# A hybrid decoder step on one core: the rotation in pieces of 256 columns, and the border to the feed-forward part regrouped

## The chip, the core and the metric

The kernel runs on one core of one Trainium2 chip. The metric is the device time of one execution in microseconds. Before the change it is 2496.76 us, the median of three runs (2495.86 to 2498.49). One further execution was taken with the hardware profiler; all rows below come from it.

## The reference

One layer of an autoregressive decoder, for a prompt of 1024 tokens and eight single-token samples with the same weights. Columns are tokens here: 1032 of them, cut into two halves of 516 where the halves matter. What bears on the change:

```
proj = rmsnorm(x, g_mix) @ w_in
rq, rk = rotary(rq, pos), rotary(rk, pos) * RET_DK ** -0.5     # 4 heads of 128
o_r, s_ret = retention_chunked(rq, rk, rv, s_ret)
...
x = x + merged @ w_out
x = x + cross_attn(rmsnorm(x, g_x), mk, mv, w_xq, w_xo)
h = rmsnorm(x, g_ffn)
x = x + (silu(h @ w_gate) * (h @ w_up)) @ w_down
```

`rotary` takes the two halves x1, x2 of a head's 128 channels to x1 cos - x2 sin and x1 sin + x2 cos. `rmsnorm` scales each token by 1 / sqrt(mean of squares + eps), which the kernel computes as exp(-0.5 ln(...)).

## The kernel before, in words

Every large product is made of three TensorE products: each float32 operand is split into a high part (ScalarE copies it to a shorter format, `L235`, `L253`) and a low part (the remainder, formed by VectorE or GpSimd, `L236`, `L254`). `dense` (`L252` to `L254` in `wsplit`) loads 512 KB of weights through SP's queue into a staging tile, splits it, and multiplies block by block; a function called `evac` brings each block out of PSUM.

The stages follow each other: the input projections with the gated-delta branch, then the retention branch together with projections and the memory keys and values, then `w_out` with the residual, cross attention, `w_xo` with the second residual, the feed-forward part, and the final norm. TensorE's order in the first stages is written out by hand: dense products call `tick()`, which lets threads of the other branches put in their products when a simulated clock says so. On the other engines a planner orders the instructions by a simulated timeline; every engine then works its queue in order. `tc.issue_after(ins)` ties what a block issues on the engine of `ins` behind `ins`, and nothing else.

**The rotation.** `ret_qk(h, u)` loads queries and keys of one head and one half of 512 tokens into `qk` ([128, 2, 512], `rqk` in the rows). `swapped` (`L887`) multiplies each half of the partitions by the sine rows into the other half of `w` (`rsw`), two instructions of 64 partitions; `L904` multiplies `qk` by the cosines and `L905` adds `w`. All four run on GpSimd, for 2 x 512 columns at a time, for each of eight units. Low halves of the rotated queries (`L928`) and of the scores (`L936`) are formed on GpSimd as well. Beside that VectorE carries the samples' retention and gated-delta states (`svn`, `L1151` to `L1161`), the retention state's low halves (`rS`), evacuations (`ev`, `kv`) and weight remainders.

**The tables of ScalarE.** A norm is `rsnorm`: a product with ones on TensorE (`pn`), Ln (`L315`) and Exp (`L317`) on ScalarE, block by block. ScalarE needs the table of a function loaded; `preload_act_table_set("natural_log_exp_and_others")` asks for the set that has both, once at the start (`L211`) and once ahead of `residual(w_out)` (`L1402`). The latter has no operands, so nothing ties its place in ScalarE's order.

**The border to the feed-forward part.** `residual_half(c, ms)` (`L1545` on) multiplies by `w_xo`, tile by tile of 128 rows, for half c of the tokens. Its evacuation adds the old x (`L1558`), stores the sum, squares it (`L1561`), adds the squares up on GpSimd (`L1563`) and multiplies x by the gain in place (`L1564`), which waits for the store. The feed-forward products use a seven-product scheme on quarters: `xr[r][c]` is rows half r, token half c, as two tiles each. `scale(r, c)` (`L1571`) multiplies a quarter by the norm `rsB`, two instructions of 128x1032. `operands(p, ...)` splits the sums or differences that product p needs.

```
        residual_half(0, range(KT))
        rsnorm(rsB, sqx, D, halves_of(0))
        residual_half(1, range(2))
        with tc.issue_after(taken[0].ins):      # the last evacuation traced
            scale(0, 0)
        operands(1, r2tile, quarters(0, 0))
        scale(1, 0)
        operands(2, r2tile, quarters(1, 0))
        residual_half(1, range(2, KT))
```

`Pair(ft)` is one tile of 128 hidden rows: it loads gate and up weights (`wg`, `wu`; `wraw` takes the staging tile from the rotating list `stage`), forms sums of their quarters on GpSimd (`L1687`, numbers 5, 6, 7 and, last, 3, which overwrites the sum of number 6), and `product(p)` splits the weights and issues 24 TensorE products and their evacuations (`L1717` to `L1736`). Tiles 0 and 1 run their products in the order 1, 2 (tile 0), 1, 2 (tile 1), 7, 7, 5, 6, 6, 4, 4, 3, 5, 3. Behind the first of these the second half's norm is issued; then the quarters of half 1 are scaled (`L1773`), their difference `xt3` for product 7 is formed (`L1774`), and the further differences (`L1779`) and operands follow, all ahead of product 7 in the program. Tiles 2 to 21 follow with all seven products each.

Of the kernel before, what the change touches and what calls it, by code (L numbers as in the profile page):

```python
# [9 lines left out]
F32 = mybir.dt.float32  # L10
F32R = mybir.dt.float32r
AF = mybir.ActivationFunctionType
ALU = mybir.AluOpType
# [4 lines left out]
P = 128  # L18
# [4 lines left out]
KT = D // P  # L23
# [3 lines left out]
H = NT // 2  # L27
# [116 lines left out]
def build(tc, io):  # L144
    nc = tc.nc
    ve, se, ge = nc.vector, nc.scalar, nc.gpsimd
# [19 lines left out]
    with ExitStack() as es:  # L166
# [11 lines left out]
        wp = pool("wp", 2)  # L178
# [49 lines left out]
        def r1tile(name, dt=F32R):  # L228
            return r1p.tile([P, NT], dt, name=name, tag="r1")
# [13 lines left out]
        stage = [wp]  # L243
# [640 lines left out]
        def swapped(w, t, r):  # L884

            for o, i in ((slice(0, 64), slice(64, P)), (slice(64, P), slice(0, 64))):
                ge.tensor_tensor(w[o], t[i], r[i], op=ALU.mult)  # L887
# [8 lines left out]
        def ret_qk(h, u):  # L896
            n = f"{h}_{u}"
            cs = slice(u * 512, u * 512 + 512)
            qk = rp.tile([P, 2, 512], F32, name=f"rqk{n}", tag="rqk", bufs=2)
            w = rp.tile([P, 2, 512], F32, name=f"rsw{n}", tag="rsw")  # L900
            load(qk, rqkd[:, h:h + 5:4, cs], h + u == 1)
            rots = [rot[:, j, cs].unsqueeze(1).to_broadcast([P, 2, 512]) for j in range(2)]
            swapped(w, qk, rots[1])
            ge.tensor_tensor(qk, qk, rots[0], op=ALU.mult)  # L904
            ge.tensor_tensor(qk, qk, w, op=ALU.add)  # L905
            return qk

        def ret_v(h, u):
# [490 lines left out]
                one(m)  # L1399
            return oh, ol  # L1400

        se.preload_act_table_set("natural_log_exp_and_others")  # L1402
        sqx = e2.tile([P, NT], F32, name="sqx", tag="sqx", bufs=1)
        xh, xl = residual(io["w_out"], gh, gl_, lambda m: io["xT"][:, m], x1d, G_X, lambda m: r2tile, sqx, "x1")
        rsB = cp.tile([P, NT], F32, name="rsB1", tag="rsB")
# [133 lines left out]
        def pair(new, name, dt=F32R):  # L1539
            return new(name, dt).rearrange("p (i t) -> p i t", i=2)  # L1540
# [39 lines left out]
        def operands(p, new, srcs):  # L1580
            xo[p] = []
            for j, s in enumerate(srcs):
                t = pair(new, f"xo{p}_{j}")
                split(t[:, 0], t[:, 1], s)
                xo[p].append(t)
# [1 line left out]
        quarters = lambda r, c: [quarter(r, c, j) for j in range(4)]  # L1587
        residual_half(0, range(KT))
        rsnorm(rsB, sqx, D, halves_of(0))
        residual_half(1, range(2))  # L1590

        with tc.issue_after(taken[0].ins):
            scale(0, 0)
        operands(1, r2tile, quarters(0, 0))
        scale(1, 0)
        operands(2, r2tile, quarters(1, 0))
        residual_half(1, range(2, KT))
        ast.close()

        pss.close()  # L1600
# [8 lines left out]
        def ftile(tag, name, shape, bufs=1, dt=F32):  # L1609
            return fp.tile(shape, dt, name=name, tag=tag, bufs=bufs)  # L1610

        stage[:] = [wp, fp, fp, fp]
        nop = [0]

        def wop(name):
# [49 lines left out]
        class Pair:  # L1665


            def __init__(self, ft):
                self.ft = ft
                wg, wu = wraw(f"wg{ft}"), wraw(f"wu{ft}")  # L1670
                dma(out=wg, in_=io["w_gate"][ft])
                flush(dma(out=wu, in_=io["w_up"][ft]))
                a11, a12, a21, a22 = wg[:, :4], wg[:, 4:], wu[:, :4], wu[:, 4:]
                s1, s2 = (ftile(f"S{i}", f"S{i}_{ft}", [P, 4, P], 2) for i in (1, 2))
                self.srcs = {1: a11, 2: a12, 3: s2, 4: a22, 5: s1, 6: s2, 7: a21}
                self.sums = {5: (s1, a21, a22, ALU.add), 6: (s2, s1, a11, ALU.subtract), 7: (a21, a11, a21, ALU.subtract),
                             3: (s2, a12, s2, ALU.subtract)}
                self.at, self.seen = {}, []
                self.t = r1tile(f"hid{ft}", F32)
                up = ev if ft % 2 else e1  # L1680
                self.U = [up.tile([P, BLK], F32, name=f"U{ft}_{i}", tag="ev" if ft % 2 else "gt")[:, :H // 2] for i in range(2)]

            def weights(self, p):
                for q in {6: (5, 6), 7: (5, 7), 5: (5,), 3: (5, 6, 3)}.get(p, ()):
                    if q in self.sums:
                        o, x, y, op = self.sums.pop(q)
                        ge.tensor_tensor(o, x, y, op=op)  # L1687
                w = wop(f"w{p}_{self.ft}")
                split(*w, self.srcs[p])
                return w  # L1690
# [75 lines left out]
        f1 = Pair(1)  # L1766
        for p in (1, 2):
            f1.product(p)
        xt3 = [pair(r1tile, f"xt3{i}", F32) for i in range(2)]
        for i in range(2):  # L1770
            for r in (1, 0):
                e = xr[r][1][i]
                ve.tensor_tensor(e, e, rsB[:, half(1)].unsqueeze(1).to_broadcast([P, 2, H]), op=ALU.mult)  # L1773
            ve.tensor_tensor(xt3[i], xr[1][1][i], xr[0][1][i], op=ALU.subtract)  # L1774
        operands(7, r2tile, [xt3[j // 2][:, j % 2] for j in range(4)])
        for p, new, (r, c) in ((5, r2tile, (0, 1)), (6, r1tile, (0, 1)), (4, r1tile, (1, 0))):
            for i in range(2):
                x, y = (xr[r][c][i], xr[0][0][i]) if p == 5 else (xr[1][1][i], xr[0][1][i]) if p == 6 else (xr[1][0][i], xr[0][1][i])
                ve.tensor_tensor(xr[r][c][i], x, y, op=ALU.subtract)  # L1779
            operands(p, new, quarters(r, c))  # L1780
        operands(3, r1tile, quarters(1, 1))
        for f, p in ((f0, 7), (f1, 7), (f0, 5), (f0, 6), (f1, 6), (f0, 4), (f1, 4), (f0, 3), (f1, 5), (f1, 3)):
            f.product(p)
        f0.done()
        f1.done()
# [143 lines left out]
```

## Time and profile before, and how to read it

| | |
|---|---|
| median of three runs | 2496.76 us |
| the profiled execution | 2501.62 us |
| its span, first to last instruction | 2499.8 us |
| mean granted TensorE clock | 0.986 |
| instructions | 44199 |
| busy: TensorE / VectorE / ScalarE / GpSimd | 2401.3 / 1518.8 / 978.2 / 897.6 us |
| read from HBM, written | 243.91 MB, 97.78 MB |

PE is TensorE, DVE VectorE, ACT ScalarE, POOL GpSimd, SPq the queue of loads and stores. Products are pipelined, so TensorE's busy time counts overlaps, and a busy TensorE is not one at its peak; the granted clock (PEclk, 1.00 is 2.4 GHz, 0.50 is 1.2 GHz) says how fast it could run. `L157` is the line of every TensorE product, so products are told apart by their tiles: `pd` is a dense product, `P` one of the feed-forward scheme, `pks`, `pro`, `prs` are of the retention stage, `pn` is a norm. A wait is given as idle time of the engine and what released it.

### The profile page before, as it was taken

How to read it: one execution, taken by the hardware profiler on the slowest of the kernel's cores; microseconds unless marked ns; L12 is line 12 of the kernel's file. 1: busy time of each engine (PE TensorE's matmuls, PEld its weight loads, DVE VectorE, ACT ScalarE, POOL GpSimd, SP SyncE). 2: the span in 40 equal slices, each digit the busy share in tenths (PEclk: the TensorE clock that was granted, in tenths of full speed). 3: DMA queues.
4: the chain of work that ended last, by engine and by line, in shares of the span. 5: the costliest groups of instructions: out<-in, count | busy, mean ns of one | idle time of the engine just before them, and what ended most of it. 6: DMA issues, size and time to landing. Idle time of an engine off the chain costs nothing. (4 is left out here: it accounts for less than half of the span.)

```text
span 2499.8 us, 44199 instructions
## 1 busy us (share of the span) xinstructions
PE 2401.3 (96%) x17290; PEld 2314.2 (93%) x17290; DVE 1518.8 (61%) x2957; ACT 978.2 (39%) x1757; POOL 897.6 (36%) x846
## 2 busy tenths in 40 slices
PE   8999999999999999898999999998889999999998
PEld 6999999999999998788999999878889999999998
DVE  5866857668576536787544445342496656656665
ACT  4333243433424333564422343234543333335453
POOL 4344243343434327442001120003388655620233
PEclk9999999999999999999999999999989999999999
DMA  4222222222222236577666543335345445438654
GB/s 145 87 68 72 89 89 85 72 74 86 82 84 76 83 112 197 194 227 233 212 184 177 157 135 102 124 126 177 107 136 189 162 131 170 140 126 286 211 157 150
DMA packets 201090, 344.60 MB, mean 138 GB/s; under 512 B 39984, under 2 KB 125488, under 8 KB 200752
## 3 DMA queue, kind: packets, MB, share of 16 engines
q1 hardware_dynamic: 200880, 341.76, 43.5%
q8 instruction: 136, 2.23, 0.4%
q14 instruction: 74, 0.61, 0.1%
HBM read 243.91 MB, written 97.78 MB: 137 GB/s over the span
## 5 line engine op out<-in xcount | busy, mean ns | idle before, releaser
L157 PE MATMUL pd<-x0h,wh 128*128 128x344 f32 (+1 forms) x1712 | 575.9, 338 | 10.5 <-ACT x0h L238 5.5
L157 PE MATMUL pd<-x0h,wl 128*128 128x344 f32 (+1 forms) x1712 | 548.8, 322 | 0.0
L157 PE MATMUL pd<-x0l,wh 128*128 128x344 f32 (+1 forms) x1712 | 547.7, 321 | 0.4 <-DVE x0l L239 0.4
L157 PE MATMUL P<-xo,w 128*128 128x258 f32 x3696 | 453.2, 285 | 15.0 <-ACT xo L235 7.8
L157 PEld LDWEIGHTS P<-xo,w 128*128 128x128 f32 x3696 | 451.3, 192 | 16.6 <-ACT xo L235 8.4
L157 PEld LDWEIGHTS pd<-x0h,wh 128*128 128x128 f32 (+1 forms) x1712 | 323.2, 189 | 20.0 <-DVE ev L361 6.1
L157 PEld LDWEIGHTS pd<-x0l,wh 128*128 128x128 f32 (+1 forms) x1712 | 323.3, 189 | 1.9 <-DVE x0l L239 0.8
L157 PEld LDWEIGHTS pd<-x0h,wl 128*128 128x128 f32 (+1 forms) x1712 | 322.7, 189 | 1.2
L253 ACT ACTIVATE wh<-wf 128x1024 fp32r<-128x1024 f32 (+1 forms) x137 | 144.0, 1052 | 269.2 <-PE pd L157 180.9
L157 PE MATMUL D<-ho,wd 128*128 128x258 f32 x1584 | 192.3, 284 | 2.9 <-ACT ho L235 2.9
L157 PEld LDWEIGHTS D<-ho,wd 128*128 128x128 f32 x1584 | 191.8, 190 | 3.2 <-ACT ho L235 3.1
L254 POOL TENSOR_TENSOR wl<-wf,wh 128x1024 fp32r<-128x1024 f32 x60 | 144.5, 2408 | 52.0 <-ACT wh L253 51.0
L254 DVE TENSOR_TENSOR wl<-wf,wh 128x1024 fp32r<-128x1024 f32 (+1 forms) x77 | 102.7, 1333 | 54.1 <-ACT wh L253 53.8
L361 DVE TENSOR_TENSOR ev<-pd,rsB 128x344 f32<-128x344 f32 x140 | 71.1, 508 | 62.1 <-PE pd L157 56.4
L236 DVE TENSOR_TENSOR wd<-wd,wd 128x512 fp32r<-128x512 f32 (+1 forms) x96 | 67.5, 708 | 53.2 <-ACT wd L235 52.0
L706 DVE TENSOR_TENSOR tm<-Ab,px 128x16 f32<-128x16 f32 (+30 forms) x248 | 72.4, 292 | 34.7 <-POOL Ab L703 30.0
L236 DVE TENSOR_TENSOR w<-S,w 128x512 fp32r<-128x512 f32 x66 | 64.5, 977 | 41.8 <-ACT w L235 41.8
L1364 POOL TENSOR_TENSOR ma<-ma,my 128x344 f32<-128x344 f32 x24 | 22.3, 929 | 181.6 <-DVE ma L1363 166.0
L235 ACT ACTIVATE wd<-wd 128x512 fp32r<-128x512 f32 (+1 forms) x96 | 56.5, 591 | 73.5 <-PE D L157 51.9
L157 PE MATMUL pd<-oh,wh 128*128 128x258 f32 x256 | 75.2, 294 | 8.1 <-DVE xr L1558 6.0
L235 ACT ACTIVATE w<-S 128x512 fp32r<-128x512 f32 x66 | 41.6, 630 | 93.9 <-PE P L157 81.4
L157 PE MATMUL pd<-oh,wl 128*128 128x258 f32 x256 | 74.8, 293 | 2.4 <-DVE wl L254 2.4
(765 smaller groups left out, 5405.4 us busy)
## 6 DMA issues: line engine op xcount, KB each, us to landing
wf<-w_in SPq DMA_DIRECT2D x72, 512.0 KB, 3.6
wu<-w_up SPq DMA_DIRECT2D x22, 512.0 KB, 4.1
wg<-w_gate SPq DMA_DIRECT2D x22, 512.0 KB, 3.6
sd<-w_down SPq DMA_DIRECT2D x40, 256.0 KB, 4.1
wsd<-sd SPq DMA_DIRECT2D x20, 512.0 KB, 5.9
wd<-wsd SPq DMA_DIRECT2D x20, 512.0 KB, 4.2
kc<-ck SPq DMA_DIRECT2D x32, 256.0 KB, 3.8
vc<-cv SPq DMA_DIRECT2D x32, 256.0 KB, 3.5
```

The lines of the kernel that those rows point to most:

```text
L157: return nc.tensor.matmul(out, lhsT=lhsT, rhs=rhs, **kw)
L235: se.activation(hi, src, AF.Copy)
L236: return ve.tensor_tensor(lo, src, hi.bitcast(F32), op=ALU.subtract)
L253: se.activation(wh[:, :kt, :m], wf, AF.Copy)
L254: wlo[0].tensor_tensor(wl[:, :kt, :m], wf, wh[:, :kt, :m].bitcast(F32), op=ALU.subtract)
L361: ve.tensor_tensor(e[:, :n], pt, rsB[:, a:b], op=ALU.mult)
L706: ve.tensor_tensor(tm[:, :, :w], Ab[:, i, :w].unsqueeze(1).to_broadcast([P, 8, w]), X[:, :, :w], op=ALU.mult)
L1364: ge.tensor_tensor(e[:, :n], e[:, :n], y[:, :n], op=ALU.add)
```

## The change

`ret_qk` works in four pieces, by queries and keys and by 256 columns, each with its own two swapped products, cosine product and sum. The second preload is tied behind what was traced before it on ScalarE. Three tiles of the second half of `w_xo`, instead of two, stand ahead of the first half's scaling in the program. The difference `xt3` is formed from the unscaled quarters right after the last residual tile, and scaled instead of the two quarters; the quarters are scaled later, ahead of the products that need them, and each product stands behind its operands in the program. The staging list starts one place on, so that the single tile of `wp` takes the up weights of odd tiles instead of the gate weights of even ones. For tiles 0 and 1 the sums 5, 6 and 7 are issued as soon as the tile is made, and sum 3 goes to VectorE.

```
@@ ret_qk
-            rots = [rot[:, j, cs].unsqueeze(1).to_broadcast([P, 2, 512]) for j in range(2)]
-            swapped(w, qk, rots[1])
-            ge.tensor_tensor(qk, qk, rots[0], op=ALU.mult)
-            ge.tensor_tensor(qk, qk, w, op=ALU.add)
+            for j in range(2):
+                for i in range(0, 512, 256):
+                    x, y = qk[:, j, i:i + 256], w[:, j, i:i + 256]
+                    r = rot[:, :, u * 512 + i:u * 512 + i + 256]
+                    swapped(y, x, r[:, 1])
+                    ge.tensor_tensor(x, x, r[:, 0], op=ALU.mult)
+                    ge.tensor_tensor(x, x, y, op=ALU.add)
@@ ahead of residual(w_out)
-        se.preload_act_table_set("natural_log_exp_and_others")
+        tc.keep_in_program_order(se.preload_act_table_set("natural_log_exp_and_others"))
@@ the border
-        residual_half(1, range(2))
+        residual_half(1, range(3))
...
-        residual_half(1, range(2, KT))
+        residual_half(1, range(3, KT))
+        xt3 = [pair(r1tile, f"xt3{i}", F32) for i in range(2)]
+        for i in range(2):
+            ve.tensor_tensor(xt3[i], xr[1][1][i], xr[0][1][i], op=ALU.subtract)
...
-        stage[:] = [wp, fp, fp, fp]
+        stage[:] = [fp, fp, fp, wp]
@@ class Pair
+                if ft < 2:
+                    self.sum(5, 6, 7)
...
-            def weights(self, p):
-                for q in {6: (5, 6), 7: (5, 7), 5: (5,), 3: (5, 6, 3)}.get(p, ()):
+            def sum(self, *qs):
+                for q in qs:
                     if q in self.sums:
                         o, x, y, op = self.sums.pop(q)
-                        ge.tensor_tensor(o, x, y, op=op)
+                        (ve if self.ft < 2 and q == 3 else ge).tensor_tensor(o, x, y, op=op)
+
+            def weights(self, p):
+                self.sum(*{6: (5, 6), 7: (5, 7), 5: (5,), 3: (5, 6, 3)}.get(p, ()))
@@ after the first products of tiles 0 and 1
-        xt3 = [pair(r1tile, f"xt3{i}", F32) for i in range(2)]
-        for i in range(2):
-            for r in (1, 0):
-                e = xr[r][1][i]
-                ve.tensor_tensor(e, e, rsB[:, half(1)].unsqueeze(1).to_broadcast([P, 2, H]), op=ALU.mult)
-            ve.tensor_tensor(xt3[i], xr[1][1][i], xr[0][1][i], op=ALU.subtract)
+        for x in xt3:
+            ve.tensor_tensor(x, x, rsB[:, half(1)].unsqueeze(1).to_broadcast([P, 2, H]), op=ALU.mult)
         operands(7, r2tile, [xt3[j // 2][:, j % 2] for j in range(4)])
-        for p, new, (r, c) in ((5, r2tile, (0, 1)), (6, r1tile, (0, 1)), (4, r1tile, (1, 0))):
+        for f in (f0, f1):
+            f.product(7)
+        scale(0, 1)
+        for p, new, (r, c), fs in ((5, r2tile, (0, 1), [f0]), (6, r1tile, (0, 1), [f0, f1]), (4, r1tile, (1, 0), [f0, f1])):
             for i in range(2):
...
             operands(p, new, quarters(r, c))
+            if p == 5:
+                scale(1, 1)
+            for f in fs:
+                f.product(p)
         operands(3, r1tile, quarters(1, 1))
-        for f, p in ((f0, 7), (f1, 7), (f0, 5), (f0, 6), (f1, 6), (f0, 4), (f1, 4), (f0, 3), (f1, 5), (f1, 3)):
+        for f, p in ((f0, 3), (f1, 5), (f1, 3)):
             f.product(p)
```

## Rows read from the trace of the kernel before

**Rows 1.** The page, busy time: us, share of the span, instructions.

```profile
PE 2401.3 (96%) x17290; PEld 2314.2 (93%) x17290; DVE 1518.8 (61%) x2957; ACT 978.2 (39%) x1757; POOL 897.6 (36%) x846
```

**Rows 2.** Windows of the retention stage: length, engines' busy us, granted clock, DMA, GB/s.

```profile
1020.00:1040.00 20.00, 16.58 (x101) 15.02 (x94) 13.31 (x27) 7.44 (x15) 9.22 (x8) 0.91 0.53 185
...
1060.00:1080.00 20.00, 17.04 (x98) 16.22 (x99) 16.43 (x41) 6.81 (x12) 8.69 (x6) 0.83 0.50 162
...
1120.00:1140.00 20.00, 13.47 (x83) 11.80 (x84) 18.59 (x23) 9.37 (x16) 12.09 (x6) 0.83 0.75 249
```

**Rows 3.** TensorE's waits, 930 to 1200 us: released by, total us, times, longest.

```profile
PE pks L157 <- DVE svn L1152: 6.1, 2, 3.9
PE pro L161 <- DVE kv L1268: 5.8, 1, 5.8
PE pro L157 <- DVE rS_0l L236: 4.5, 2, 3.4
```

**Rows 4.** Timeline of VectorE and GpSimd at 1054 to 1066 us: start, length.

```profile
1058.21 2.36 DVE L1152 TENSOR_SCALAR svn<-svn,bs 8x128 f32<-8x128 f32 x1
...
1055.57 4.91 POOL L887 TENSOR_TENSOR rsw<-rqk,rot 64x1024 f32<-64x1024 f32 x2
```

**Rows 5.** GpSimd's groups by form, 935 to 1160 us, and one row of its timeline.

```profile
L887 POOL TENSOR_TENSOR rsw<-rqk,rot 64x1024 f32<-64x1024 f32 x16 | 40.3, 2521 | 6.3 <-DMA rqk<-rqkd 5.5
...
L1257 POOL TENSOR_TENSOR sqa<-sqa,mq 128x256 f32<-128x256 f32 x1 | 0.7, 737 | 0.1
...
1113.22 1.39 POOL L928 TENSOR_TENSOR rq_1l<-rqk,rq_1h 128x512 fp32r<-128x512 f32 x1 [5.84 <-PE pks L161]
```

**Rows 6.** TensorE's waits at the border, 1680 to 1900 us.

```profile
PE P L157 <- ACT xo L235: 7.8, 3, 4.9
PE pd L157 <- DVE xr L1558: 6.0, 2, 5.7
PE P L157 <- ACT U L1717: 4.0, 1, 4.0
```

**Rows 7.** The line of Ln in the norms: engine, operation, count, ns, first and last start.

```profile
L315 ACT ACTIVATE rsB<-pn,epsc x10: 476/547/551, 37.0 to 1802.3; 128x344 f32<-128x344 f32 x6, 128x258 f32<-128x258 f32 x4
L315 ACT ACT_TABLE_LOAD  x8: 1283/1283/1283, 1106.7 to 1801.0; - x8
```

**Rows 8.** TensorE's waits, 1480 to 1680 us, the longest in total.

```profile
PE pd L157 <- DVE eq L1514: 0.9, 2, 0.7
```

**Rows 9.** First half's norm and scaling: timelines of ScalarE and VectorE, one window.

```profile
1737.32 1.28 ACT L315 ACT_TABLE_LOAD   x1
1738.62 0.48 ACT L315 ACTIVATE rsB<-pn,epsc 128x258 f32<-128x258 f32 x1
...
1744.63 0.42 ACT L317 ACTIVATE rsB<-rsB 128x258 f32<-128x258 f32 x1
...
1745.08 1.23 DVE L1571 TENSOR_TENSOR xr<-xr,rsB 128x1032 f32<-128x1032 f32 x1 [6.18 <-ACT rsB L317]
...
1747.80:1753.80 6.00, 5.95 (x27) 5.96 (x28) 1.85 (x4) 1.35 (x3) 0.74 (x1) 0.50 0.58 175
```

**Rows 10.** ScalarE's timeline at the second half's norm, first and last of nine rows.

```profile
1797.44 1.28 ACT L315 ACT_TABLE_LOAD   x1
...
1804.32 0.42 ACT L317 ACTIVATE rsB<-rsB 128x258 f32<-128x258 f32 x1
```

**Rows 11.** After that norm: one window, VectorE's groups, GpSimd's and ScalarE's timelines.

```profile
1804.50:1861.50 57.00, 46.84 (x323) 45.75 (x323) 54.55 (x73) 24.80 (x50) 40.62 (x18) 0.84 0.29 88
...
L236 DVE TENSOR_TENSOR xo<-xr,xo 128x516 fp32r<-128x516 f32 x16 | 15.5, 1003 | 0.0
...
L236 DVE TENSOR_TENSOR xo<-xt,xo 128x516 fp32r<-128x516 f32 x4 | 2.6, 693 | 0.0
...
1811.32 18.09 POOL L1687 TENSOR_TENSOR S<-wg,S 128x512 f32<-128x512 f32 x1 [14.84 <-DVE w L236]
...
1832.80 0.63 ACT L235 ACTIVATE w<-S 128x512 fp32r<-128x512 f32 x1 [5.92 <-POOL S L1687]
```

## The prediction

> **What bounds the kernel now.** The page first: TensorE is busy 96% of the span [rows 1], so there is little to win anywhere but where it stands or runs at half clock. The windows and the engine's waits show two such stretches, and the change touches both.
>
> The first is the retention stage, 935 to 1160 us. In three 20 us windows TensorE is busy 13.5 to 17.0 us, and its granted clock is 0.91, 0.83 and 0.83 [rows 2]. Three waits on VectorE make 16.4 us there [rows 3]. What holds VectorE up is seen in the timeline: the `svn` scaling at 1058.21, an 8x128 instruction, lasts 2.36 us and ends as the pair of rotation instructions on GpSimd ends (1055.57 + 4.91 = 1060.48) [rows 4]. So a VectorE instruction with SBUF inputs that meets a rotation instruction waits for the end of that instruction, and rotation instructions last 2.5 us [rows 5].
>
> The second stretch is the border, 1737 to 1862 us: 17.8 us of TensorE waits [rows 6], most of them in the steps taken up below.
>
> **The change, part by part.**
>
> *Rotation.* Per unit of head and half, four instructions of 1024 columns become sixteen of 256, on the same tiles and engine. No DMA is added; the load of a unit still stands ahead of it. Eight units, so 32 instructions become 128. The trace has a 256-column GpSimd product at 0.74 us [rows 5], so a unit grows from about 4 x 2.5 = 10 to 16 x 0.74 = 11.8 us. That is cover for VectorE: an instruction that meets a piece waits at most 0.74 instead of 2.5 us, 0.3 of it. The 16.4 us of waits would fall to about 5: gain 11.4 us. The low clock goes with the waits: 0.09 + 0.17 + 0.17 of 20 us is 8.6 us of TensorE time [rows 2]; the rotation's waits open each of the three, but other small waits remain, so I take half, 4.3. Against it: the first unit is wanted at once, and is 1.8 us longer, though its query half is ready sooner; I charge 1. Term: -14.7, taken as -14.5. Bounds: nothing, if other late work fills the gaps, to 16.4 + 8.6 = 25; the value lies nearer the middle, since the longest waits are chains of two or three blocked instructions and no single one.
>
> *The preload of the table set.* The diff pins the preload ahead of `residual(w_out)`. In the trace of before it has done nothing: from 37 us on Ln and Exp of the first norm run without loads, but from 1106.7 on the line of Ln has 8 loads of its own, as each Ln and each Exp fetches another table [rows 7]. Pinned, one load serves them. It is one instruction of 1.28 us at a point where TensorE has work; cost nothing, covered by the dense products there. If that cover were gone it would be 1.3 us.
>
> What it takes away, norm by norm: (a) the norm after `w_out`, three blocks, 6 loads. TensorE waits 0.9 us there [rows 8], which is all there is to win: -0.9. (b) The norm of the first half: the chain from 1737.32 to 1745.05 is 7.7 us, of it four loads, 5.1 [rows 9]. (c) The norm of the second half: 1797.44 to 1804.74, 7.3 us, again 5.1 of loads [rows 10].
>
> A load is followed by its activation 1.30 us after it starts (1737.32, 1738.62) [rows 9]. The Trainium skill's "ScalarE: Activation LUTs", section What ACT_TABLE_LOAD costs, adds a drain of about 1.38 us to a switch; by it the two chains would lose 10.6 us each rather than 5.1, and my sum would be some 11 us better. That gap is in neither row, so it gets no chance of its own.
>
> *First border, and `residual_half(1, range(3))`.* At 1742 TensorE waits 5.7 us for an evacuation [rows 6] that is queued on VectorE behind a scaling of x, which itself waited 6.18 us for rsB; then the clock is 0.50 for 6 us, 3.0 us lost [rows 9]. Together 8.7. The program ties only `scale(0, 0)` behind the named evacuation. The first of the two scalings in the trace comes three evacuations earlier, so it must be `scale(1, 0)`, which nothing ties. The regrouping to three tiles moves only the tied one and the operand splits, all covered by the five following tiles; what moves the stall is (b). With rsB 5.1 us earlier, the wait would be 0.6 us and the clock would hold: -8. But without loads the planner may draw `scale(1, 0)` ahead of one more evacuation, and then the stall stays: 0. I take the middle, rounded up a little, -4.5, as the two are equally near; bounds 0 and -8.7.
>
> *Second border.* After rsB VectorE is the bound: busy 54.6 of 57 us, with TensorE at clock 0.84 [rows 11]. So I count VectorE's list, and TensorE's waits inside it are not added. (c) starts the list 5.1 us earlier. The difference of the two quarters moves ahead of the norm, where VectorE has room: two instructions of 128x1032, 2.4 us by the scaling of that shape [rows 9], less from the list; in their place the two differences are scaled instead of four quarters, and the four quarters only later, between products: the number of scalings rises by two, 2.4 back on. But the first product on new operands now waits for two instructions after rsB rather than six, so TensorE starts on it while VectorE goes on. It is not counted, as the list sets the end.
>
> The two sums of tiles 0 and 1 come onto VectorE: 2 x 0.69 = 1.4, by the free remainder of that size [rows 11]. Against that, the GpSimd sum that VectorE kept out lasted 18.09 us, ScalarE's next split stood 5.92 us behind it, and TensorE waited 4.9 behind the splits that came next [rows 6, 11]; this goes, and with it most of the 2.4 us in which VectorE is not busy. VectorE's own blocking shrinks: sixteen operand remainders average 1.00 us where free ones take 0.69, 5 us over [rows 11], and GpSimd now has two sums fewer and begins the next tile's earlier, while VectorE still holds it off; I take 3 of the 5. Two remainders of the first weights can run while the norm does, 1.4.
>
> Queues: of the first tiles' loads one of 512 KB still waits on SP for the last weight buffer. It is now the up weights of tile 1 instead of the gate weights of tile 0, so the first product's split no longer waits at the head of ScalarE's queue (0.5), but tile 1's three sums wait on GpSimd, among the last squares' sums that the norm needs. In the trace three sums stand at the same place, so nothing; if they come first, up to 2 us on the norm. Late next is the difference of the last two tiles, which VectorE cannot form before their stores have landed; behind it in VectorE's queue may stand the remainders of tile 1's first weights, and TensorE for those.
>
> So 5.1 (norm) + 2.4 + 3 + 1.4 - 1.4 + 0.5 = 11: -11. Bounds: -3 (only part of the norm) to -18 (all waits of the second border, 11.8, and most of the half clock).
>
> *Sum.* -14.5 - 0.9 - 4.5 - 11 = -30.9. The profiled execution took 2501.62 us (span 2499.8), so 2470.7 for a profile; the median of the runs, 2496.76, is 4.9 below that execution, so 2466.
>
> **The rivals.**
>
> A. *The rotation pieces free nothing.* VectorE is busy 13 to 19 of 20 us in this stage, so its list itself may set the pace, and each TensorE wait removed may come back at the next transfer. For it: VectorE's business; against it: part of that business is the waiting itself. The term falls to 2: 2478.
>
> B. *The border pays little.* VectorE's list is as long as before, GpSimd's sums block it elsewhere, and the scaling still stands ahead of the evacuation. Left are the rotation, 0.9, 1 and 3: 2477.
>
> C. *Slower: the pieces starve.* The place is the rotation on GpSimd. The 18.09 us sum [rows 11] shows that GpSimd can lose turn after turn against VectorE instructions that follow each other closely; sixteen pieces must win a turn sixteen times, and behind them in GpSimd's queue stand the low halves that TensorE multiplies by. A unit takes 10 us; behind the one that ends at 1107 GpSimd is idle for 5.84 us before such a low half [rows 5]. So it decides from a piece, with its wait, of (10 + 5.8) / 16 = 0.99 us on. If each piece waits for one VectorE instruction of 1.2 us [rows 9], a unit lasts 16 x 1.94 = 31 us, 15 over that slack; three such units make 45 us, less the border's 16: 2526. Against it: in this stage rotation instructions keep close to 2.5 us on average.
>
> The Trainium skill's "SBUF — State Buffer", section Who interferes with whom, says that where VectorE reads two SBUF operands the engine that issues second waits out the other's whole instruction. By that, more pieces are more chances to lose, which is rival C, but each loss would end with one instruction; the 18 us row [rows 11] does not agree with the latter.
>
> D. *The change doesn't do what it says*: the pinned preload is overtaken by another table before the norms, and Ln and Exp load as before. Then (a), (b), (c) go: 14.5 + 0.5 + 5 remain: 2477.
>
> **How the numbers follow.** Forecast 0.62; A 0.15; B 0.11; D 0.04; A and B together 0.03, at 2490 (2 + 0.9 + 1 + 3 gained) or above, counted as within; C 0.05. A measurement of this kernel can tell about 0.2%, 5 us, from no change. Faster by more: 0.62 + 0.15 + 0.11 + 0.04 = 0.92; within: 0.03; slower: 0.05. The range holds A, B and D with some room above, 2485, and below takes the better ends of the border with the forecast of the rotation and some of its clock: 14.5 + 4 + 0.9 + 8.7 + 18 = 46, with a little left out at that end: 2451. The forecast case alone spans 2453 to 2475.
>
> **What would show it.** Right: the three waits on `svn`, `kv` and the state's low half under 1.5 us each and the clock near 1.00 from 1020 to 1140; no 2.3 us `svn`; no loads on the norm lines after `w_out`; rsB within 2.5 us of its first Ln at both halves; no wait over 4 us at 1742; no GpSimd sum over 3 us in the border; VectorE still nearly full there. Wrong: rotation units of over 16 us, new TensorE waits on GpSimd's `rqk`, or the same evacuation wait at the first border. The forecast falls if TensorE's waits go and the stage is as long as before: then VectorE's list was the bound.

## The result, and the profile after

The changed kernel takes 2470.25 us (median of four runs, 2467.87 to 2471.56) against 2497.62 us (four, 2495.86 to 2499.2): ratio 0.989, 95% interval 0.9876 to 0.9903. The forecast was 2466, the range 2451 to 2485, so the direction and the size came true. The profiled executions differ by 30.4 us (2501.62 and 2471.22); by the same working the steps made 30.9. That agreement is partly luck: the rotation and the first border gave 2.1 and 2.3 us more than forecast, the second border 6.7 us less, and 2.7 us lie in no step.

Five landmarks cut both traces into stretches. *Retention* is from the samples' rotation (`qkw`) to the first split of the merged branches (`a0h`); *w_xo* from its first to its last evacuation (`xr<-pd,xs`); *norm* from the first product `P<-xo` to VectorE's first scaling behind it; *list* from there to the start of VectorE's last `hid<-hid,V` of tile 1; *FF* from the first to the last `P<-xo` product (it contains the two before).

| us | retention | w_xo | norm | list | FF | span |
|---|---|---|---|---|---|---|
| before | 292.9 | 113.3 | 13.7 | 58.9 | 468.3 | 2499.8 |
| after | 276.3 | 106.5 | 6.7 | 60.6 | 464.0 | 2469.4 |
| difference | -16.6 | -6.8 | -7.0 | +1.7 | -4.3 | -30.4 |

The other 2.7 us of the span lie outside these stretches: 1.6 ahead of the rotation, where nothing was changed, and 1.1 between the retention and `w_xo` and at the end. From run to run these move by as much: in the traces of this case the rotation starts between 934.4 and 939.2 us.

The page, busy time, which answers to [rows 1]; TensorE's busy time fell by 12.8 us with the same 17290 products, while the granted clock over the span rose from 0.986 to 0.994:

```profile
PE 2388.5 (97%) x17290; PEld 2300.9 (93%) x17290; DVE 1504.4 (61%) x2961; ACT 961.4 (39%) x1744; POOL 901.2 (36%) x940
```

The same windows of the retention stage as in [rows 2], TensorE's waits there as in [rows 3], and GpSimd's rotation by form as in [rows 5]:

```profile
1020.00:1040.00 20.00, 19.89 (x155) 17.68 (x154) 15.22 (x46) 10.01 (x22) 11.98 (x16) 1.00 0.66 213
1060.00:1080.00 20.00, 20.00 (x146) 18.33 (x145) 16.79 (x43) 17.11 (x26) 13.44 (x16) 1.00 0.79 251
1120.00:1140.00 20.00, 17.56 (x126) 16.42 (x125) 16.75 (x34) 10.90 (x23) 10.93 (x12) 1.00 0.77 273
...
PE pd L157 <- DVE ev L361: 2.4, 1, 2.4
PE pro L161 <- DVE kv L1272: 2.3, 1, 2.3
...
PE pks L157 <- DVE svn L1156: 0.9, 2, 0.6
PE prs L157 <- POOL rqk L909: 0.9, 1, 0.9
...
L887 POOL TENSOR_TENSOR rsw<-rqk,rot 64x256 f32<-64x256 f32 x64 | 52.2, 815 | 9.2 <-DMA rqk<-rqkd 5.6
L908 POOL TENSOR_TENSOR rqk<-rqk,rot 128x256 f32<-128x256 f32 x32 | 28.1, 905 | 0.6
L909 POOL TENSOR_TENSOR rqk<-rqk,rsw 128x256 f32<-128x256 f32 x32 | 24.4, 793 | 0.0
```

The three waits of 16.4 us are down to 3.2 (`rS_0l` no longer stands among the longest), and the clock is 1.00 in all three windows. One dip is left between them, 0.91 from 1040 to 1060 us. GpSimd pays: 104.7 us of rotation instead of 80.9, 13.1 us a unit. Only 0.9 us of that is a wait of TensorE, a new one, for `rqk` at 950.7 us: the first unit's.

The norms. First the line of Ln in the norms, as in [rows 7], and the load of the tied preload itself; then ScalarE and VectorE at the first half's norm, as in [rows 9], and at the second half's, as in [rows 10]:

```profile
L315 ACT ACTIVATE rsB<-pn,epsc x10: 458/534/549, 37.0 to 1770.8; 128x344 f32<-128x344 f32 x6, 128x258 f32<-128x258 f32 x4
L315 ACT ACT_TABLE_LOAD  x1: 1283/1283/1283, 1089.7 to 1089.7; - x1
L1406 ACT ACT_TABLE_LOAD  x1: 1283/1283/1283, 1381.8 to 1381.8; - x1
...
1717.22 0.46 ACT L315 ACTIVATE rsB<-pn,epsc 128x258 f32<-128x258 f32 x1
1719.27 0.40 ACT L317 ACTIVATE rsB<-rsB 128x258 f32<-128x258 f32 x1
1719.70 2.38 DVE L1575 TENSOR_TENSOR xr<-xr,rsB 128x1032 f32<-128x1032 f32 x2 [0.79 <-ACT rsB L317]
...
1769.99 0.47 ACT L315 ACTIVATE rsB<-pn,epsc 128x258 f32<-128x258 f32 x1
1771.31 0.42 ACT L317 ACTIVATE rsB<-rsB 128x258 f32<-128x258 f32 x1
1771.77 2.38 DVE L1782 TENSOR_TENSOR xt<-xt,rsB 128x1032 f32<-128x1032 f32 x2 [0.91 <-ACT rsB L317]
```

The second preload now loads its set at 1381.8 us, ahead of the norm behind `w_out`; in the trace of before no load stands on its line. The norms' own loads from `w_out` on are gone (the one left on the Ln line, at 1089.7, is of the memory keys' norm), the chains are 2.45 and 1.74 us long instead of 7.7 and 7.3, and VectorE waits 0.79 us for the first half's `rsB` instead of 6.18. At half 0 two ScalarE instructions of other work stand between.

TensorE's waits at the border, as in [rows 6]; its wait ahead of the cross attention, as in [rows 8]; and one window and one group of VectorE over the list, as in [rows 11]:

```profile
PE P L157 <- DVE xo L236: 4.2, 3, 3.4
...
PE P L157 <- DVE w L236: 3.2, 1, 3.2
PE P L157 <- ACT xo L235: 2.7, 1, 2.7
PE pd L157 <- DVE xr L1562: 2.0, 5, 0.7
...
PE pd L157 <- DVE eq L1518: 0.9, 2, 0.7
...
1771.50:1832.50 61.00, 47.48 (x341) 44.97 (x341) 57.56 (x79) 27.24 (x54) 24.96 (x16) 0.89 0.26 83
...
L236 DVE TENSOR_TENSOR xo<-xr,xo 128x516 fp32r<-128x516 f32 x16 | 17.3, 1127 | 0.0
```

The evacuation's wait of 5.7 us is gone (longest now 0.7), and the granted clock is 1.00 from 1715 to 1732 us, around the first half's scaling. Past the norm nothing was won: VectorE is busy 57.6 of 61.0 us (before, over the same stretch, 56.0 of 59.2), so its idle time is as it was, and the sixteen operand remainders became longer, 1127 ns instead of 1003. What runs beside them is seen in the timelines of VectorE and GpSimd:

```profile
1800.83 10.32 DVE L236 TENSOR_TENSOR xo<-xr,xo 128x516 fp32r<-128x516 f32 x8
...
1790.92 4.32 POOL L1696 TENSOR_TENSOR S<-wu 128x512 f32<-128x512 f32 x1 [21.76 <-DMA wu<-w_up]
...
1803.68 1.18 POOL L1664 TENSOR_TENSOR sd<-sd 128x256 f32<-128x256 f32 x1
...
1811.70 1.19 POOL L1667 TENSOR_TENSOR sd<-sd 128x256 f32<-128x256 f32 x1
```

Eight remainders take 10.32 us, where four free ones take 2.50 (at 1741.10), and beside them GpSimd forms eight sums of quarters of `w_down` without a gap (first and last shown), 1.07 to 1.19 us each. In the trace of before the same eight stood later, from 1843.71 on, 39 us into the list instead of 32, where single remainders and evacuations run.

### The profile page after: what moved, and what is told of

Its sections match the earlier page's. It is cut to its first block, busy times and chain, and to the rows that moved or that the text cites. A ratio compares the mean times of both kernels' runs of the same rounds, so it can differ in the third digit from the quotient of the medians.

```text
span 2469.4 us, 44298 instructions
## 1 busy us (share of the span) xinstructions
PE 2388.5 (97%) x17290; PEld 2300.9 (93%) x17290; DVE 1504.4 (61%) x2961; ACT 961.4 (39%) x1744; POOL 901.2 (36%) x940
## 5 line engine op out<-in xcount | busy, mean ns | idle before, releaser
L236 DVE TENSOR_TENSOR w<-S,w 128x512 fp32r<-128x512 f32 x66 | 60.6, 919 | 39.3 <-ACT w L235 39.3
L707 DVE TENSOR_REDUCE px<-tm 128x8 f32<-128x16 f32 (+30 forms) x248 | 73.8, 298 | 5.0
```

The lines of the kernel that those rows point to most:

```text
L236: return ve.tensor_tensor(lo, src, hi.bitcast(F32), op=ALU.subtract)
L707: ve.tensor_reduce(X[:, :, i], tm[:, :, :w], axis=AX.X, op=ALU.add, negate=True)
```

## The experiments

The same landmarks for every run. "Ratio" is to runs of the kernel before on the same chip, with its 95% interval; the stretches are of the profiled execution, one for each kernel. So it matters how far a stretch scatters between kernels that do the same in it: retention from 274.7 to 278.1 in the nine with pieces of 256, `w_xo` from 104.8 to 106.7 with the tie and from 110.2 to 113.3 without it (in either order of the border), the list from 58.8 to 58.9 in the four with the old order and from 60.4 to 62.1 in the six with the new one (e9, e13, e14 and e15 apart).

| kernel | median us | ratio | retention | w_xo | norm | list | FF |
|---|---|---|---|---|---|---|---|
| changed kernel | 2470.25 | 0.9890 (0.9876 to 0.9903) | 276.3 | 106.5 | 6.7 | 60.6 | 464.0 |
| e1 pieces alone | 2481.33 | 0.9939 (0.9915 to 0.9962) | 278.1 | 111.9 | 13.6 | 58.8 | 468.1 |
| e2 preload alone | 2483.18 | 0.9951 (0.9932 to 0.9970) | 291.9 | 105.4 | 7.5 | 58.8 | 462.0 |
| e3 regrouping alone | 2497.87 | 1.0007 (0.9996 to 1.0018) | 293.8 | 111.5 | 12.1 | 60.6 | 469.5 |
| e4 all but the preload | 2481.42 | 0.9949 (0.9933 to 0.9966) | 277.1 | 110.2 | 11.7 | 62.1 | 470.6 |
| e5 pieces of 512 | 2475.48 | 0.9917 (0.9900 to 0.9934) | 280.0 | 106.7 | 6.3 | 60.6 | 463.7 |
| e6 pieces of 128 | 2474.62 | 0.9916 (0.9896 to 0.9935) | 281.0 | 105.5 | 6.3 | 60.4 | 462.3 |
| e12 pieces and preload | 2469.28 | 0.9892 (0.9874 to 0.9910) | 274.7 | 105.2 | 7.4 | 58.9 | 462.0 |
| e10 scalings tied | 2470.06 | 0.9890 (0.9875 to 0.9906) | 274.7 | 105.7 | 6.3 | 60.8 | 462.9 |
| e9 late `w_down` sums | 2463.91 | 0.9868 (0.9852 to 0.9883) | 274.9 | 105.5 | 6.3 | 56.2 | 459.3 |
| e13 = e12, late sums | 2464.86 | 0.9875 (0.9857 to 0.9892) | 275.4 | 104.8 | 7.4 | 56.4 | 459.6 |
| e14 = e9, sum 3 on GpSimd | 2471.29 | 0.9896 (0.9878 to 0.9914) | 276.3 | 105.1 | 6.6 | 62.7 | 465.8 |
| e15 = e13, sum 3 on VectorE | 2463.80 | 0.9870 (0.9853 to 0.9887) | 276.6 | 105.1 | 7.4 | 56.1 | 458.6 |

**One part at a time.** e1 is the kernel before with the pieces alone:

```
+            for j in range(2):
+                for i in range(0, 512, 256):
+                    ...
```

> Of the change, only the rotation in pieces of 256 columns. Theory, from the two traces: up to the first use of the retention output the kernel after is ahead by 18.2 us, of it 1.6 before the rotation starts, so the pieces alone are worth 16 to 17 us: 2481, with the three waits on svn, kv and the state's low half down from 16.4 us to under 5. Rival: the stage gained by the planner's other order in the kernel after and the pieces alone bring under 10: 2488 or more.

Measured 2481.33 us. The retention lost 14.8 us and the stretches at the border are those of before, with the evacuation's wait in its place:

```profile
PE pd L157 <- DVE xr L1562: 6.0, 2, 5.7
...
PE pro L161 <- DVE kv L1272: 2.1, 1, 2.1
```

e2 is the kernel before with the preload tied:

```
-        se.preload_act_table_set("natural_log_exp_and_others")
+        tc.keep_in_program_order(se.preload_act_table_set("natural_log_exp_and_others"))
```

> Of the change, only the pinned preload. Theory (VectorE's list after the second norm sets the end of the border): both norms lose 5.1 us of loads, the first border gains 6 to 7 as in the kernel after, the second starts its list 5 to 7 earlier and gains that: together 11 to 14, 2485. Rival 1 (the GpSimd sum of 18 us sets the second border, not the list): the second border gains 2 or less, together 7 to 9, 2490. Rival 2 (the first border needs three tiles ahead of the scaling): it gains nothing there, 2490 as well, but with the evacuation wait of 5.7 us still in the trace.

Measured 2483.18 us. One line takes 7.9 us from `w_xo` and 6.2 from the second half's norm. The evacuation's wait is gone without any regrouping, and the 18 us sum on GpSimd is still there:

```profile
PE pd L157 <- DVE xr L1558: 0.7, 2, 0.4
...
1793.24 18.08 POOL L1687 TENSOR_TENSOR S<-wg,S 128x512 f32<-128x512 f32 x1 [9.29 <-DVE w L236]
```

e3 is the changed kernel with the rotation and the preload put back, so the regrouping alone:

```
-                for i in range(0, 512, 256):
...
-        tc.keep_in_program_order(se.preload_act_table_set("natural_log_exp_and_others"))
+        se.preload_act_table_set("natural_log_exp_and_others")
```

> The change without the pieces and without the pinned preload: only the regrouped border with the two sums on VectorE. Theory: the list on VectorE is as long as before (61.0 us in the kernel after, 59.3 before, from the first scaling to the last evacuation of tile 1), so the regrouping by itself is worth between 2 faster and 3 slower: 2496 to 2501. Rival (the regrouping itself shortens the second border, and the preload gave the first alone): 4 to 8 faster, 2490 to 2494.

Measured 2497.87 us, no change (the interval holds 1). The evacuation's wait stays, and a wait on ScalarE's split of the weights takes the place of what the new order removed:

```profile
PE pd L157 <- DVE xr L1558: 5.9, 2, 5.7
PE P L157 <- ACT w L235: 5.6, 1, 5.6
```

e4 is the changed kernel without the tie (the second half of that edit alone):

> The change with the preload left untied as before. Theory: it loses what the preload gave, 6 to 7 at the first border and 5 to 7 at the second, so 11 to 14 over the kernel after: 2481 to 2484, with eight loads on the norm lines at the border again. Rival (the regrouping does what the preload does at one of the two places): 5 to 7 over it, 2476.

Measured 2481.42 us, as e1: with late norms the pieces are all that is left. So the tie is worth 11.2 us in the changed kernel (2470.25 against 2481.42) and 13.5 in the kernel before (2483.18 against 2496.69 on the same chip).

e12 is the kernel before with the pieces and the tie, both edits above:

> The kernel before with the two parts that paid alone: the rotation in pieces of 256 columns and the table's preload kept in its place; the border as in the kernel before (range(2), all weight remainders on GpSimd, ten products behind the operands). If the parts simply add, 2497.6 - 15.4 - 13.5 = 2468.7 us, within 0.1% of the changed kernel's 2470.3 or 1 to 3 us under it, since alone the regrouping moved the first border by +1 and the second by +2 us. If the regrouping pays once the norm is early (VectorE's idle time and GpSimd's 18 us sum taken away, as the prediction had it, some 6 us), this run is slower than the changed kernel: 2475 to 2478 us. In the trace the GpSimd sum of 18 us ahead of the second border should still be there under both.

Measured 2469.28 us: the parts add, and without a line of the regrouping the time is that of the changed kernel. The long GpSimd sum (number 3 of tile 0) is in place, and it does hold TensorE up, though not directly: behind it in GpSimd's queue stand sum 5 of tile 2 and sum 3 of tile 1 (1.71 us each), ScalarE's split waits 5.89 us for the last of them, and the operand splits that TensorE needs stand behind that split:

```profile
1776.27 18.07 POOL L1691 TENSOR_TENSOR S<-wg,S 128x512 f32<-128x512 f32 x1 [9.29 <-DVE w L236]
...
1798.93 14.45 PE L157 MATMUL P<-xo,w 128*128 128x258 f32 x106 [5.28 <-ACT xo L235]
```

**The size of a piece.** e5 and e6 are the changed kernel with 512 and 128 where it has 256:

```
-                for i in range(0, 512, 256):
+                for i in range(0, 512, 512):
```

> The changed kernel with the rotation in pieces of 512 columns (each half of a pair by itself) where it has 256. If what costs is that VectorE's short operations stand still for as long as one GpSimd operation lasts, a piece of some 1.3 us gives back part of the gain: TensorE's waits on svn, kv and rS_0l in the retention, 16.4 us together before and 3 after, come to 5 to 9 us, and the time to 2473 to 2479 us. If the gain was another (other GpSimd work that got between the pieces, or any first cut is enough), within 1.5 us of the changed kernel, 2469 to 2472 us, with half the extra work of the pieces (some 12 us of GpSimd's 24) saved.

> The changed kernel with pieces of 128 columns: twice the instructions, some 0.46 us each (the 128x128 sum took 457 ns), so 32 of them or 15 us a unit against 13.1 us. If VectorE's standstill goes with the length of a piece and GpSimd keeps up, the waits left in the retention (kv 2.3, svn 0.9 us) shrink by 1 to 2 us: 2468 to 2470 us. If GpSimd's extra 1.5 to 2 us a unit are no longer hidden, the products wait for rqk (0.9 us in the changed kernel) by 1 to 2 us in each of the eight units: 2475 to 2486 us.

Measured 2475.48 and 2474.62 us: both lose to 256, 512 clearly (its fastest run, 2474.59, lies above the changed kernel's slowest, 2471.56), 128 less so (its fastest is 2471.25, and the ratios' intervals overlap), though its retention stretch lies outside the scatter of 256. For 512 (first two rows) the standstill theory holds: `svn` waits 2.6 us, between 6.1 and 0.9. For 128 (last two) neither expectation held as written. The waits on `svn` and `kv` together shrink by 0.9 us, but the units take 16.7 us, and the one wait on `rqk` grows from 0.9 to 3.4 us: again the first unit's, at 950.7 us, one of eight and not all.

```profile
L887 POOL TENSOR_TENSOR rsw<-rqk,rot 64x512 f32<-64x512 f32 x32 | 44.3, 1384 | 7.2 <-DMA rqk<-rqkd 5.5
...
PE pks L157 <- DVE svn L1156: 2.6, 2, 1.7
...
L887 POOL TENSOR_TENSOR rsw<-rqk,rot 64x128 f32<-64x128 f32 x128 | 68.5, 535 | 11.6 <-DMA rqk<-rqkd 4.1
...
PE prs L157 <- POOL rqk L909: 3.4, 1, 3.4
```

The instruction that the prediction began with gives the price of one standstill. The `svn` scaling by its tile, shortest, median and longest ns, at 512, 256 and 128 columns (2358 was the longest before), and what ran beside the longest at 128 (VectorE, GpSimd):

```profile
L1156 DVE TENSOR_SCALAR svn<-svn,bs x8: 265/288/1276, 983.8 to 1050.6; 8x128 f32<-8x128 f32 x8
...
L1156 DVE TENSOR_SCALAR svn<-svn,bs x8: 268/366/742, 984.7 to 1050.7; 8x128 f32<-8x128 f32 x8
...
L1156 DVE TENSOR_SCALAR svn<-svn,bs x8: 266/462/1304, 986.9 to 1053.6; 8x128 f32<-8x128 f32 x8
...
1051.93 1.30 DVE L1156 TENSOR_SCALAR svn<-svn,bs 8x128 f32<-8x128 f32 x1
...
1051.22 1.94 POOL L940 TENSOR_TENSOR rsc_1l<-rsc,rsc_1h 128x512 fp32r<-128x512 f32 x1
```

Down to 256 the longest halves with the piece. At 128 it is 1304 ns again, and there it ends as a GpSimd instruction that is not of the rotation ends (1051.22 + 1.94 = 1053.16), the low half of the scores, 512 columns wide: shorter pieces leave that one as it was.

**What sets the length of the list.** e10 is the changed kernel with its last four scalings tied where the source writes them:

```
+        with tc.issue_after(behind7.ins):        # the last remainder of operand 7
             scale(0, 1)
...
+                with tc.issue_after(behind5.ins):
                     scale(1, 1)
```

> The changed kernel with its last four scalings tied behind the remainders of operand 7 (two of them) and of operand 5 (two), where the source writes them; in its trace they ran ahead of both, 18.6 us of VectorE before the first remainder that a product waits for. If the length of VectorE's list alone sets the end of the border, within 1.5 us of the changed kernel (2469 to 2472 us), with TensorE's waits of 3.2, 2.7 and 3.4 us moved but not gone. If the order does (operands 7 are late by the scalings), TensorE's waits early in the border go and 3 to 6 us are won: 2464 to 2467 us.

Measured 2470.06 us, the changed kernel's time; the list is 60.8 us. Where on the list these four scalings stand does not matter here.

e9 takes the eight `w_down` sums out of the list's company, behind GpSimd's last difference of a pair of tiles:

```
                     for o, x, y in (...):
-                        ge.tensor_tensor(o, x, y, op=ALU.subtract)
+                        held[0] = ge.tensor_tensor(o, x, y, op=ALU.subtract)
...
                 if self.ft > 1 and chunks:
+                    with tc.issue_after(held[0].ins):
                         for _ in range(...):
                             down_weights(*chunks.pop(0))
```

> The changed kernel with the same one edit (w_down's sums on GpSimd behind its last difference of the first tiles). In the changed kernel the four remaining scalings and the remainders run from 1774 to 1835 us with VectorE busy 53.5 of 57 us, and the products of xr with xr take 1127 ns against 1003 ns before. If the eight sums of 1.18 us (9.4 us) are what lengthened them, 2465 to 2467 us and that mean falls back towards 1003 ns. If the lengthening comes from the f sums or from the order of the list, 2469 to 2471 us.

Measured 2463.91 us; the list is 4.4 us shorter and FF 4.7, and its slowest run (2465.68) lies under the changed kernel's fastest (2467.87). Of the 4.4 us the sixteen remainders give 3.5 (17.3 to 13.8 us); their mean falls below that of before, and the first of the `w_down` sums now starts at 1832, behind the list:

```profile
L236 DVE TENSOR_TENSOR xo<-xr,xo 128x516 fp32r<-128x516 f32 x16 | 13.8, 912 | 0.0
...
1832.07 1.88 POOL L1665 TENSOR_TENSOR sd<-sd 128x256 f32<-128x256 f32 x2
```

e13 makes the same edit in e12, with the old order of the border:

> e12 with GpSimd's weight sums for w_down (eight of some 1.2 us, that stand in the second border amid VectorE's list) issued behind the last difference that GpSimd forms of the tiles' results, so that none stands beside VectorE's remainders in the border. If these sums stretch VectorE's list (its sums of two SBUF operands and GpSimd's block each other), the second border loses 2 to 5 us: 2464 to 2467 us. If VectorE's list is as long without them, 2468 to 2470 us, as e12. If w_down's weights are then late, a new wait stands at the down projection and the time is over e12's.

Measured 2464.86 us, 4.4 under e12 in the medians, 2.5 in the list. The ratio's interval overlaps with that of e12, as e9's does with the changed kernel's, so the medians alone would not carry it; what carries it is that both lists come out shorter by more than lists scatter, and that none of the stretches ahead of them does. There is no wait at the down projection that e12 lacks.

e14 is e9 with sum 3 of the first two tiles back on GpSimd:

```
-                        (ve if self.ft < 2 and q == 3 else ge).tensor_tensor(o, x, y, op=op)
+                        ge.tensor_tensor(o, x, y, op=op)
```

> e9 (w_down's sums late) with the two third weight sums of the first tiles back on GpSimd. If the border's end is set by VectorE's list alone, the two sums of 0.68 us come off it: 2462 to 2463.5 us. If GpSimd's sums beside the list lengthen it by as much as they take themselves (two more of 1.3 us or longer, with the remainders beside them at over 1 us), nothing or a loss: 2464 to 2468 us. If GpSimd's sum is starved for some 18 us again and its weights come too late, a new wait of TensorE over 3 us on w stands at the end of the border.

Measured 2471.29 us, 7.4 over e9. The third expectation came true in the main: the sum is starved, for 13.36 us, and a new wait of TensorE appears, on `xo` and not on `w`. The chain has five links. The load of tile 2's gate weights takes the staging tile that the starved sum reads, so it is issued as that sum ends, at 1793.32, and the load of its up weights behind it. GpSimd's next sum, number 5 of tile 2, waits for these. Sum 3 of tile 1 stands behind that one and is done at 1800.83. ScalarE's split waits 12.10 us for it, at the head of ScalarE's queue, and the operand splits that TensorE needs stand behind that (timelines of GpSimd, SPq, GpSimd, ScalarE, TensorE):

```profile
1779.94 13.36 POOL L1697 TENSOR_TENSOR S<-wg,S 128x512 f32<-128x512 f32 x1 [11.51 <-DVE w L236]
...
1793.32 0.33 SPq L1679 DMA_DIRECT2D wg<-w_gate  x1
...
1798.35 1.26 POOL L1697 TENSOR_TENSOR S<-wu 128x512 f32<-128x512 f32 x1 [5.05 <-DMA wu<-w_up]
1799.57 1.26 POOL L1697 TENSOR_TENSOR S<-wg,S 128x512 f32<-128x512 f32 x1
...
1800.86 0.63 ACT L235 ACTIVATE w<-S 128x512 fp32r<-128x512 f32 x1 [12.10 <-POOL S L1697]
...
1802.07 0.80 PE L157 MATMUL P<-xo,w 128*128 128x258 f32 x2 [10.86 <-ACT xo L235]
```

VectorE stands for 9.35 us of that as well, so here its list is not what sets the end.

e15 gives e13 that one line of the regrouping, sum 3 on VectorE, and nothing else of it:

> e13 (pieces, pinned preload, late w_down sums, the border's order as before) with the third weight sum of the first two tiles on VectorE: the one line of the regrouping that e14 showed to matter, without the rest. In e13 GpSimd's sum takes 18.08 us at 1777.96, ScalarE waits 5.90 us for it and TensorE 5.28 us right behind. If that sum holds ScalarE and through it the operands, these two waits go and the second border gets 3 to 5 us shorter: 2460 to 2462 us, the shortest of all. If VectorE's list sets the end all the same, its two more sums of 0.68 us come on top or the wait moves elsewhere: 2464 to 2467 us.

Measured 2463.80 us, e13's time. The 5.28 us wait went, and another sum is starved in its place, number 5 of tile 2, for which neither ScalarE nor TensorE waits. TensorE's three waits early in the list are those of e13 (1.98, 1.54 and 2.08 us; there 1.98, 1.51 and 1.34), and behind them six of 0.4 to 0.9 us stand where e13 has one. Over the list TensorE waits 9.4 us instead of 10.6:

```profile
1780.66 15.21 POOL L1692 TENSOR_TENSOR S<-wu 128x512 f32<-128x512 f32 x1 [13.38 <-DVE w L236]
...
1782.39 10.93 PE L157 MATMUL P<-xo,w 128*128 128x258 f32 x70 [2.08 <-DVE xo L236]
```

The list is 56.1 us against 56.4, with VectorE busy 54.0 and 53.4 us of it. In the old order the end is set by VectorE's list and not by that wait. e9, e13 and e15, at 2463.8 to 2464.9 us, beat the kernel before by 1.3% and the changed kernel by some 6 us; e13 has none of the regrouping, e15 one line of it. The other parts of the regrouping (three tiles ahead, the difference formed early, the staging list, the early sums) were not taken apart.

## Why the prediction was right, and where it was not

**Rotation, -14.5: right.** 16.6 in the changed kernel, 14.8 in e1's trace. Both terms came: over the retention stretch TensorE's idle time fell by 12.6 us (22.1 to 9.4; forecast 11.4) and its busy time, which the low clock lengthens, by 4.0 (270.9 to 266.9; forecast 4.3). The first repeats, 8.1 to 9.8 us of idle time in the nine traces with pieces of 256; the second does not, 265.3 to 270.1 us at a mean granted clock of 1.00 to 0.98, so that the 4.3 was met is in part luck. The reason holds too: the dose runs (292.9 us of retention at 1024 columns, 280.0 at 512, 276.3 at 256) follow the length of one GpSimd instruction. The price of a unit was set too low, 13.1 us and not 11.8. Only the first unit's shows, as the prediction had it: it charged 1 us, and TensorE waits 0.9 us for it. At 128 columns that wait is 3.4 us.

**Norm behind `w_out`, -0.9: not seen.** The loads went, and `eq` is waited for 0.9 us as before, so that wait had not been theirs.

**First border, -4.5: mechanism right, too small.** e2 shows that the preload alone does it (-7.9), as the prediction said; e3's `w_xo` is 1.8 us shorter, where the kernel before and e1, with the same border, are 1.4 apart, and the evacuation's wait is still in its trace. The two cases between which the middle was taken were not equally near: the scaling still ran ahead of the evacuations, but with `rsB` early VectorE stands 0.79 us. The better end, -8, was the right value.

**Second border, -11: the step that failed.** The norm gave more than its 5.1 (7.0; e2 has 6.2 by the tie alone). The failure is in the terms behind it: "2.4" for VectorE's idle time, "3 of the 5" for its blocking by GpSimd, 1.4 for the two remainders that run early, less 1.4 for the two sums, together -5.4. The list grew by 1.7 us instead, and 1.0 us more was lost behind it. VectorE's idle time stayed (3.4 us of 61.0, 3.2 of 59.2). No more weight remainders ran ahead of the list than before: it holds sixteen in both traces. Its blocking grew: in the new order the `w_down` sums fall on eight remainders in a row, and e9 shows that they cost 4.4 us there (2.5 in the old order, e13). And the wait that was to be removed was none of the list's length: e12 has it and is as fast. Sum 3 on VectorE is not useless, but it repairs what the new order makes worse (e14: +7.4 without it, because the next tile's loads then wait for the starved sum); order and repair cancel.

**The sum.** -14.5 - 0.9 - 4.5 - 11 stands against -16.6, 0, -6.8, -4.3 and 2.7 that belong to no step. The rest of the miss, 4 us in the median, is the offset: the profile before lay 4.9 us above the median shown, the one after lies 1.0 above its own, and the prediction carried the 4.9 over.

**The rivals.** A fell with the retention (over the stretch VectorE's busy time fell from 209.0 to 190.2 us together with the waits: the business was partly the waiting). B was half right: the first border paid in full, the second no more than its norm, for the reason B gave, that GpSimd's sums block VectorE elsewhere. C did not come: a unit takes 13.1 us, under the 15.8 that it named as the limit; e6, at 16.7 a unit, is past it, and there the wait on `rqk` reaches 3.4 us. D fell with the single load.

**The marks.** `kv` at 2.3 us missed its 1.5, and one sum of 4.32 us missed the 3 in the border; the other marks of "right" came as written, if 0.99 on average from 1020 to 1140 us is near 1.00. Of the marks of "wrong" one came, in small: the 0.9 us wait on `rqk` is new, and it is what the prediction charged for the first unit.

The Trainium skill's "ScalarE: Activation LUTs", section What ACT_TABLE_LOAD costs, adds a drain to each load; as an estimate from its figures each chain would have lost 10.6 us by it. In the rows the chains lost 5.3 and 5.6, the four loads of 1.28 us and little more. The drain is not seen here.

## What to carry to other kernels

Where a short VectorE instruction waits for a long GpSimd one, cut the long one; cut until GpSimd's own length shows in a wait, and no further. An instruction without operands (here a table preload) is tied to its place by nothing, so look in the trace whether it did its work; it was worth nearly as much as the rotation (13.5 and 15.4 us, each alone). When VectorE's list sets an end, look at what GpSimd does beside it before reordering the list: moving that work behind the list was worth 4 to 6 us, the new order nothing.

## What was not expected of the hardware

One sum on GpSimd lasted 13.36 us in e14, 15.21 in e15 and 18.07 to 18.09 in the kernel before, e1, e2, e12 and e13, beside VectorE instructions that follow each other without a gap; a sum of that shape takes 1.26 us at 1799.57 in e14. The Trainium skill's "SBUF — State Buffer", section SBUF: two separate sides, has whichever of the two starts first hold the shared port pair for its whole instruction, and the other blocked until then. Here GpSimd's sum is blocked by many VectorE instructions in turn, some twenty in the kernel before.

The traces also show what ended it. In the kernel before, the 18.09 us end at 1829.41, 1.24 us after VectorE starts this instruction, the first in all that time that takes one of its inputs from PSUM:

```profile
1828.17 0.42 DVE L1729 TENSOR_TENSOR V<-P,V 128x258 f32<-128x258 f32 x1
```

Thirteen of the fourteen traces have such a sum, of 4.13 to 18.09 us, and in each it ends 1.21 to 1.24 us after the first VectorE instruction with an input in PSUM, which is about what a free sum takes. In the fourteenth, e14, it ends 1.1 us after VectorE runs out of work. So the sum appears to have done its work only then; no run moved such an instruction to try it.

In the other direction VectorE's loss is bounded by one GpSimd instruction, as `svn` shows at 1024, 512 and 256 columns. And the long sum cost time only where a load or another engine's queue waited on what stood behind it: 7.4 us in e14, nothing in e15.
